# Block 1 linear attention: unpadded queries, 64-row score products in two banks, both token tiles per level

## The chip, the cores and the metric

The kernel runs on one core of a Trainium2 chip. The metric is device microseconds for one call, as a median over runs. Weights and activations come from HBM, and every large product is done in three passes over a high and a low part of its float32 operands.

## The reference, cut to what matters

The model is one block of 256 tokens with a linear-attention mixer, followed by two blocks of softmax attention and SwiGLU. The change is in the first block, in its two linear attentions: `hgrn2` with 4 heads of 64 channels and `gla` with 4 heads of 32 channels, whose values have 64 channels each. Both call this function, with `CHUNK` = 64:

```python
def chunked_gated_linear_attention(q, k, v, log_f):
    # S_t = diag(f_t) S_{t-1} + k_t v_t^T ; o_t = S_t^T q_t, chunkwise
    def step(state, inp):
        qi, ki, vi, gi = inp
        cum = jnp.cumsum(gi, axis=2)
        diff = cum[:, :, :, None, :] - cum[:, :, None, :, :]
        decay = jnp.where(causal, jnp.exp(jnp.where(causal, diff, 0.0)), 0.0)
        scores = jnp.einsum('bhid,bhijd,bhjd->bhij', qi, decay, ki)
        ...
f = lb + (1.0 - lb) * jax.nn.sigmoid(z)                          # hgrn2: log_f = log f
log_f = jax.nn.log_sigmoid((g_lr @ w_g_up + b_g)) / 16.0         # gla: g_lr has 16 columns
```

So the score of query i and key j is the sum over channels of q·k·exp(cum_i − cum_j), for j ≤ i. Beside it the block has an RG-LRU mixer (a convolution of 4 taps, two block-diagonal products, a scan), output gates, and one output projection `w_out` over all three.

## The kernel before, in words

The 256 tokens are two tiles of 128. Channels lie on partitions: `fqz`, `fk` and `cum` hold queries, keys and the running sums of log f (scans, L940) in three blocks of 128 channels, f = 0 and 1 with two `hgrn2` heads each, f = 2 with the four `gla` heads. `fqz` has one slot for each of the 8 heads, with zeros in the channels of the other heads, so that a product over all 128 rows sums over one head alone.

The kernel has no chunk state. It builds the whole triangle of scores `S` for each tile from products that each have a reference time in the middle: for the half-block sizes s = 1, 2, 4, ..., 64 (levels `li` 0 to 6) every block of 2s tokens gives queries of its second half times exp(cum − cum at the middle), and keys of its first half times the inverse. A level of a tile (`level`, called tile-level below) is one subtraction `E` (L1047, GpSimd), two exponentials (ScalarE), the keys `kq` (L1059 or L1062, GpSimd), three queries `qs` (L1067 twice, L1069, VectorE), and products on TensorE (L1073) into one PSUM bank. The four smallest levels multiply all 128 keys by 64 queries and pick what counts by `copy_predicated` into `S` (L1078, VectorE); the others multiply block by block and ScalarE copies (L1081). `diagonal` (L1028, L1030) gives i = j, `across` the queries of tile 1 times the keys of tile 0. `outputs` multiplies `S` by the values (L1104, L1105), norms, gates and transposes.

The order is written by hand as a string, `plan`: `v`, `af`, `cq`, `c`, `lru`, `g`, `o` are projections and the LRU mixer; two digits are a level and a tile; X, D, O are `across`, `diagonal`, `outputs`. `weave` starts a unit at each mark and moves all that are alive one `yield` on. A scheduler then merges the engines' streams by this priority. PSUM has four single banks `mm_t` in a ring, two `acc_t` (projections, convolution, LRU), two `tp_t`. Weights come by `piece`: a load on SP's queue into one of four `raw` buffers, a high part on ScalarE (L108), a low part `wl_t` on VectorE or GpSimd (L111), nine buffers each. A convolution's three taps (L958) read the `acc_t` of its projection, so the bank is free only after the last tap. `evac` copies PSUM out by ScalarE and VectorE in turn. At the end `contract` multiplies by `w_out` in the order [2, 3, 0, 1] of its four pieces, adds, norms (`rms_norm`), and the gated MLP (`gv1` weights) follows.

Of the kernel before, what the change touches and what calls it, by code (L numbers as in the profile page):

```python
# [69 lines left out]
class Net:  # L70
    POOL_SHARE = 3

    def __init__(self, ctx, tc, io):
# [756 lines left out]

    def mixers1(self, mix, post):
# [64 lines left out]
        def af():  # L896
            ks, n = group("af")
            ps = [self.mm.tile([P, 2, T], F32, name="mm_t") for _ in range(2)]
# [16 lines left out]
        def cq():
            ks, n = group("cq")
            ps = self.mm.tile([P, 2, T], F32, name="mm_t")
# [6 lines left out]
            ps = self.mm.tile([P, T], F32, name="mm_t")  # L924
# [3 lines left out]
            ps = self.mm.tile([P, T], F32, name="mm_t")  # L928
# [87 lines left out]
        def scaled(E, q):  # L1016
            w = E.shape[2]
            qa, qc = self.t2(4, w, name="qa"), self.t2(4, w, name="qc")
            v.tensor_tensor(qa.rearrange("p (b j) t -> p b j t", b=2), q[:, 0:4, :].rearrange("p (b j) t -> p b j t", b=2),
                            E[:, 0:2, :].unsqueeze(2).broadcast_to([P, 2, 2, w]), ALU.mult)  # L1020
            v.tensor_tensor(qc, q[:, 4:8, :], E[:, 2:3, :].broadcast_to([P, 4, w]), ALU.mult)
            return qa, qc

        def products(ksrc, qa, qc):
# [6 lines left out]
            return pa, pc  # L1031

        def diagonal(t):
            tsl = slice(t * P, (t + 1) * P)
            ps = products(fk[:, :, tsl], fqz[:, 0:4, tsl], fqz[:, 4:8, tsl])
            yield
            for i, p_ in enumerate(ps):
                v.tensor_tensor(S[:, t, 4 * i : 4 * i + 4, :], p_, self.ident.unsqueeze(1).broadcast_to([P, 4, P]), ALU.mult)

        def level(t, li):  # L1040
            s = LEVELS[li]
            tsl = slice(t * P, (t + 1) * P)
# [23 lines left out]
            for b in range(2):
                v.tensor_tensor(qv[:, 2 * b : 2 * b + 2], q2[:, 2 * b : 2 * b + 2],  # L1067
                                E2[:, b : b + 1].broadcast_to([P, 2, nb, s]), ALU.mult)
            v.tensor_tensor(qv[:, 4:8], q2[:, 4:8], E2[:, 2:3].broadcast_to([P, 4, nb, s]), ALU.mult)  # L1069
            ps = self.mm.tile([P, 8, 64], F32, name="mm_t")  # L1070
            for rows, cols in blocks:
                for f, h0, h1 in ((0, 0, 2), (1, 2, 4), (2, 4, 8)):
                    nc.tensor.matmul(ps[rows, h0:h1, cols], lhsT=kq[:, f, rows], rhs=qs[:, h0:h1, cols],  # L1073
                                     start=True, stop=True)
            yield
            if li < MASKED:
                mk = masks[:, li, :].rearrange("p (b u) -> p b u", u=s).unsqueeze(1).broadcast_to([P, 8, nb, s])
                v.copy_predicated(second(S[:, t]), mk, blk(ps))  # L1078
            else:
                for b, (rows, cols) in enumerate(blocks):  # L1080
                    act.activation(second(S[rows, t])[:, :, b], ps[rows, :, cols], AF.Copy)  # L1081

        def across():
            Eq, Ek = (mix.tile([P, 3, P], F32, name="E", bufs=3) for _ in range(2))
# [4 lines left out]
            kq = mix.tile([P, 3, P], F32, name="kq", bufs=3)  # L1089
            g.tensor_tensor(kq, fk[:, :, 0:P], Ek, ALU.mult)  # L1090
            qa, qc = scaled(Eq, fqz[:, :, P:T])
            ps = products(kq, qa, qc)
            yield
            for i, p_ in enumerate(ps):
                self.evac(SX[:, 4 * i : 4 * i + 4, :], p_)

# [37 lines left out]
        for tok in plan.split():
            if tok in F:
                seq.append(F[tok])
            elif tok in "|-":
                seq.append(None)
            elif tok[0] in U:
                seq += [[U[tok[0]](int(tok[1]))], None]  # L1140
            else:
# [314 lines left out]
```

## Time and profile before

| | us |
|---|---|
| median of 3 runs (1338.17 to 1339.03) | 1338.34 |
| the profiled execution, its own time | 1337.82 |
| its span | 1336.0 |
| TensorE busy in the span | 1296.4 (97%) |
| VectorE busy | 887.6 (66%) |
| ScalarE busy | 729.7 (55%) |
| GpSimd busy | 560.1 (42%) |

The profiled execution takes 1.82 us more than its span (launch and end). Its own time is 0.52 us under the median. Times below count from the span's start. PE is TensorE's matmul, PEld its weight load, DVE VectorE, ACT ScalarE, POOL GpSimd. Block 1's mixers take roughly the first 150 us of the span.

### The profile page before, as it was taken

The page shows a single profiled execution, that of the slowest core. Times are in us where ns is not written, and L with a number is a line of the kernel's source. Part 1 is how long each engine was busy: PE and PEld are TensorE (multiplying, and loading weights), DVE is VectorE, ACT ScalarE, POOL GpSimd, SP SyncE. Part 2 cuts the span into 40 slices and gives each one's busy share as a digit, 9 for nine tenths or more (in the row PEclk, how much of TensorE's full clock was granted, in tenths as well). Part 3 has the DMA queues.
Part 4 walks back from the last instruction along what each step waited for, and adds up shares of the span by engine and source line. Part 5 has one row for each costly group of instructions (what it writes and reads, how often), then busy time and mean ns, then how long its engine had stood idle before and what let it go on. Part 6 is the DMA issues. An engine that isn't in the chain of part 4 may idle for free.

```text
span 1336.0 us, 19335 instructions
## 1 busy us (share of the span) xinstructions
PE 1296.4 (97%) x7028; PEld 1092.1 (82%) x7028; DVE 887.6 (66%) x1402; ACT 729.7 (55%) x1282; POOL 560.1 (42%) x542
## 2 busy tenths in 40 slices
PE   8888999999999999999999999999999999999997
PEld 6767788888888887877888888888887877888886
DVE  5798588863577636587767745677726678777734
ACT  5775466654555543475565543555533666565540
POOL 5563433333444435830534444334436831444430
PEclk9999999999999999999999999999999999999999
DMA  6523555575655564550665565655664540655560
GB/s 221 190 64 124 183 164 187 188 221 156 222 188 186 189 205 134 182 173 1 191 218 188 187 208 152 211 190 189 221 190 129 168 157 1 221 191 188 189 205 32
DMA packets 63922, 227.19 MB, mean 170 GB/s; under 512 B 7105, under 2 KB 8145, under 8 KB 63058
## 3 DMA queue, kind: packets, MB, share of 16 engines
q1 hardware_dynamic: 63826, 225.95, 52.7%
q8 instruction: 55, 0.90, 0.3%
q14 instruction: 41, 0.34, 0.1%
HBM read 224.88 MB, written 1.05 MB: 169 GB/s over the span
## 4 chain that ended last, share of the span: by engine, by line
PE 80%; POOL 6%; DVE 5%; issue 3%; DMA 3%; ACT 2%; SPq 0%; DVEq 0%; ACTq 0%; POOLq 0%
PE mm_t L347 38%; PE acc_t L214 5%; PE acc_t L208 5%; PE acc_t L211 5%; PE mm_t L214 3%; PE mm_t L211 3%; PE mm_t L208 3%; PE mm_t L133 3%; PE mm_t L131 3%; PE mm_t L132 3%; POOL wl_t L111 3%; PE tp_t L149 2%; PE mm_t L431 1%; PE mm_t L684 1%; PE acc_t L131 1%
## 5 line engine op out<-in xcount | busy, mean ns | idle before, releaser
L111 POOL TENSOR_TENSOR wl_t<-raw,wh_t 128x512 fp32r<-128x512 f32 (+3 forms) x270 | 408.6, 1536 | 576.8 <-ACT wh_t L108 570.6
L111 DVE TENSOR_TENSOR wl_t<-raw,wh_t 128x1024 fp32r<-128x1024 f32 (+2 forms) x272 | 391.2, 1445 | 239.8 <-ACT wh_t L108 238.9
L108 ACT ACTIVATE wh_t<-raw 128x1024 fp32r<-128x1024 f32 (+2 forms) x407 | 416.5, 1039 | 222.8 <-PE mm_t L214 135.1
L347 PE MATMUL mm_t<-xx,wh_t 128*128 128x512 f32 x1456 | 429.0, 395 | 0.0
L347 PEld LDWEIGHTS mm_t<-xx,wl_t 128*128 128x128 f32 x1456 | 247.9, 188 | 47.4
L347 PE MATMUL mm_t<-xx,wl_t 128*128 128x256 f32 x1456 | 261.4, 281 | 0.0
L347 PEld LDWEIGHTS mm_t<-xx,wh_t 128*128 128x128 f32 x1456 | 236.2, 189 | 15.7
L350 DVE TENSOR_TENSOR sum<-sum,mm_t 128x256 f32<-128x256 f32 x182 | 75.4, 414 | 38.0 <-ACT sum L349 37.9
L349 ACT ACTIVATE sum<-mm_t 128x256 f32<-128x256 f32 x182 | 67.9, 373 | 43.0 <-PE mm_t L347 43.0
L208 PE MATMUL mm_t<-wh_t,hh 128*128 128x512 f32 x218 | 85.2, 391 | 0.0
L211 PE MATMUL mm_t<-wl_t,hh 128*128 128x512 f32 x218 | 84.8, 389 | 0.0
L211 PE MATMUL acc_t<-wl_t,hh 128*128 128x512 f32 x218 | 84.8, 389 | 0.0
L208 PE MATMUL acc_t<-wh_t,hh 128*128 128x512 f32 x218 | 84.8, 389 | 0.0
L131 PE MATMUL mm_t<-wh_t,xx 128*128 128x512 f32 (+2 forms) x224 | 83.8, 374 | 0.8 <-ACT xx L125 0.7
L132 PE MATMUL mm_t<-wl_t,xx 128*128 128x512 f32 (+2 forms) x224 | 83.0, 371 | 0.0
L133 PE MATMUL mm_t<-wh_t,xx 128*128 128x512 f32 (+2 forms) x224 | 82.0, 371 | 0.0
L125 ACT ACTIVATE hh<-ht 128x256 fp32r<-128x256 f32 x72 | 30.1, 418 | 85.4 <-DVE ht L294 85.4
L214 PE MATMUL acc_t<-wh_t,hl 128*128 128x512 f32 x218 | 71.8, 389 | 0.0
L214 PE MATMUL mm_t<-wh_t,hl 128*128 128x512 f32 x218 | 68.1, 389 | 0.0
L131 PE MATMUL acc_t<-xx,wh_t 128*128 128x256 f32 x176 | 52.2, 297 | 5.0 <-ACT wh_t L108 2.8
L126 DVE TENSOR_TENSOR hl<-ht,hh 128x256 fp32r<-128x256 f32 x72 | 37.9, 526 | 22.1 <-ACT hh L125 22.1
L132 PE MATMUL acc_t<-xx,wh_t 128*128 128x256 f32 x176 | 50.8, 289 | 0.0
(336 smaller groups left out, 2046.0 us busy)
## 6 DMA issues: line engine op xcount, KB each, us to landing
raw<-in_wgu_dram SPq DMA_DIRECT2D x176, 512.0 KB, 4.4
raw<-in_wd_dram SPq DMA_DIRECT2D x109, 512.0 KB, 4.4
raw<-in_gv_dram SPq DMA_DIRECT2D x42, 512.0 KB, 4.5
raw<-in_w_in_dram SPq DMA_DIRECT2D x36, 512.0 KB, 4.4
raw<-in_wo_dram SPq DMA_DIRECT2D x24, 512.0 KB, 3.8
gb<-in_ln_dram SPq DMA_DIRECT2D x6, 1024.0 KB, 4.7
raw<-in_w_in_dram SPq DMA_DIRECT2D x16, 384.0 KB, 3.6
raw<-in_w_in_dram SPq DMA_DIRECT2D x8, 416.0 KB, 3.6
```

What stands on the lines that cost most here:

```text
L108: nc.scalar.activation(hv, raw, AF.Copy)
L111: eng.tensor_tensor(lv[:, x : x + m], raw[:, x : x + m], hv.bitcast(F32)[:, x : x + m], ALU.subtract)
L126: self.nc.vector.tensor_tensor(dst_l, src, dst_h.bitcast(F32), ALU.subtract)
L131: mm(out, lhsT=lhs[0], rhs=rhs[0], start=start, stop=False, **kw)
L132: mm(out, lhsT=lhs[0], rhs=rhs[1], start=False, stop=False, **kw)
L133: mm(out, lhsT=lhs[1], rhs=rhs[0], start=False, stop=stop, **kw)
L208: m = self.nc.tensor.matmul(ps[t][h], lhsT=lh, rhs=wh[:, sl], start=first, stop=False)
L211: self.nc.tensor.matmul(ps[t][h], lhsT=lh, rhs=wl[:, sl], start=False, stop=False)
L214: self.nc.tensor.matmul(ps[t][h], lhsT=ll, rhs=wh[:, sl], start=False, stop=last)
L347: nc.tensor.matmul(out, lhsT=lhsT, rhs=rhs, start=k == 0 and i == 0, stop=k == NK - 2 and i == 3)
L349: nc.scalar.activation(r, ps[:, 1, :], AF.Copy)
L350: nc.vector.tensor_tensor(r, r, ps[:, 0, :], ALU.add)
```

## The change

Queries become `fq` with 4 slots: a slot holds two heads, one on channels 0 to 63 and one on channels 64 to 127 (a `gla` head still has zeros beside it in its 64). `products` runs each score product on 64 rows, the upper and the lower half in turn, and writes the halves' results into the two banks of a double tile (`double`; two of them in the ring, in place of four single banks, for block 1). `level` handles both tiles: one `E`, one `kq` and two `qs` for 256 tokens, all on VectorE, then products per tile. `kq` lives in two fixed buffers that are zeroed once. The heads leave `outputs` in another order. `af` evacuates with one copy in place of two, and the load of `consts` moves ahead on SP's queue. The plan is a new string.

```diff
+    def double(self):
+        return self.mm.tile([P, 2, 512], F32, name="mm_t")
...
-        fqz = mix.tile([P, 8, T], F32, name="fqz")
+        fq = mix.tile([P, 4, T], F32, name="fq")
-        v.memset(fqz, 0.0)
+        v.memset(fq[:, 2:4, :], 0.0)
+        kqs = [mix.tile([P, 3, T], F32, name=f"kq{i}") for i in range(2)]
+        for kq in kqs:
+            g.memset(kq, 0.0)
...
-            fqv = fqz[:, 0:4, :].rearrange("p (b j) t -> p b j t", b=2)
-            for r in range(2):
-                a = slice(r * 64, r * 64 + 64)
-                self.evac(fqv[a, :, r, :], ps[0][a])
+            self.evac(fq[:, 0:2, :], ps[0])
...
-                self.evac(fqz[a, 4 + h, :], ps[a, 0, :], 32.0 ** -0.5)
+                self.evac(fq[a, 2 + h % 2, :], ps[a, 0, :], 32.0 ** -0.5)
...
-            for j in range(2):
-                nc.tensor.matmul(pa[:, 2 * j : 2 * j + 2, :], lhsT=ksrc[:, j, :], rhs=qa[:, 2 * j : 2 * j + 2, :],
-                                 start=True, stop=True)
-            nc.tensor.matmul(pc, lhsT=ksrc[:, 2, :], rhs=qc, start=True, stop=True)
+        FS = ((0, 0, 1), (1, 1, 2), (2, 2, 4))
+        def products(ps, ksrc, qsrc, rows=slice(0, P), cols=slice(0, P)):
+            for f, s0, s1 in FS:
+                for r in range(2):
+                    a = slice(r * 64, r * 64 + 64)
+                    nc.tensor.matmul(ps[rows, 4 * r + s0 : 4 * r + s1, cols], lhsT=ksrc[a, f, rows], rhs=qsrc[a, s0:s1, cols],
+                                     start=True, stop=True)
+        def heads():
+            return self.double().rearrange("p b (s c) -> p (b s) c", s=4)
+        def scale(out, q, E):
+            v.tensor_tensor(out[:, 0:2], q[:, 0:2], E[:, 0:2], ALU.mult)
+            v.tensor_tensor(out[:, 2:4], q[:, 2:4], E[:, 2:3].broadcast_to([P, 2, *E.shape[2:]]), ALU.mult)
...
-        def level(t, li):
+        def level(li):
-            g.tensor_tensor(E.rearrange("p f (b u) -> p f b u", u=2 * s), c4d,
-                            c4d[:, :, :, s - 1 : s].broadcast_to([P, 3, nb, 2 * s]), ALU.subtract)
+            E = mix.tile([P, 3, T], F32, name="E", bufs=3)
+            v.tensor_tensor(view(E), c4d, c4d[:, :, :, s - 1 : s].broadcast_to([P, 3, NT * nb, 2 * s]), ALU.subtract)
...
+            self.nkq += 1
+            kq = kqs[self.nkq % 2]
+            qs = mix.tile([P, 4, P], F32, name="qs", bufs=3)
+            v.tensor_tensor(first(kq), first(fk), first(E), ALU.mult)
+            scale(blk(qs), second(fq), second(E))
...
+            for t in range(NT):
+                ps = heads()
+                for rows, cols in blocks:
+                    products(ps, kq[:, :, t * P : (t + 1) * P], qs[:, :, t * 64 : (t + 1) * 64], rows, cols)
...
-            g.tensor_tensor(Ek, cum[:, :, 0:P], cum[:, :, P - 1 : P].broadcast_to([P, 3, P]), ALU.subtract)
+            v.tensor_tensor(Ek, cum[:, :, 0:P], cum[:, :, P - 1 : P].broadcast_to([P, 3, P]), ALU.subtract)
...
-        plan = ("v0 af cq X0 c0 D0 v1 40 c3 60 c1 c2 lru 50 30"
-                " | 20 00 g0 10 O0 D1 o0 61 31 41 o1 51 11 o2 g1 o3 21 01 O1")
+        plan = "v0 af cq X0 c0 D0 D1 v1 L4 c3 L6 c1 c2 lru L5 L3 | L2 g0 L0 o0 L1 o1 g1 O0 o2 O1 o3"
...
+        mm1 = ExitStack()
+        self.mm = mm1.enter_context(tc.tile_pool(name="mm1", bufs=2, space=PSUM))
...
+        mm1.close()
+        self.mm = self.ctx.enter_context(tc.tile_pool(name="mm", bufs=4, space=PSUM))
         tc.keep_in_program_order(nc.sync.dma_start(ctile, io["consts"]))
```

TensorE of the kernel before, where the gate's small matmul stands (`mm_t_531<-glr`, from which the `gla` decays come) among the projections of convolution 0 (`acc_t_577`) and of the values of tile 1 (`acc_t_622`):

```order
L132 MATMUL acc_t_622<-wl_t_142,xx_94 128x512
L133 MATMUL acc_t_622<-wh_t_141,xx_94 128x512
L131 MATMUL acc_t_622<-wh_t_149,xx_94 128x512
L133 MATMUL acc_t_577<-xx_94,wl_t_567 128x256
L131 MATMUL acc_t_577<-xx_94,wh_t_573 128x256
L929 MATMUL mm_t_531<-glr_529,gup_196 128x256
L132 MATMUL acc_t_577<-xx_94,wh_t_573 128x256
L133 MATMUL acc_t_577<-xx_94,wl_t_574 128x256
```

TensorE after, at the same matmul, now among the projections of convolution 3 (`acc_t_667`), with products of the diagonal (`mm_t_606`) behind it:

```order
L131 MATMUL acc_t_667<-xx_91,wh_t_566 128x256
L132 MATMUL acc_t_667<-xx_91,wl_t_567 128x256
L130 MATMUL acc_t_667<-xx_91,wh_t_566 128x256
L131 MATMUL acc_t_667<-xx_91,wh_t_566 128x256
L936 MATMUL mm_t_531<-glr_529,gup_195 128x256
L1030 MATMUL mm_t_606<-fq_252,fk_253 128x128 x4
L1030 MATMUL mm_t_606<-fq_252,fk_253 128x256 x2
L132 MATMUL acc_t_667<-xx_91,wl_t_567 128x256
L130 MATMUL acc_t_667<-xx_91,wh_t_573 128x256
L131 MATMUL acc_t_667<-xx_91,wh_t_573 128x256
```

The gate's matmul now has 33 more projection matmuls ahead of it on TensorE than before (22 of 128x256, 11 of 128x512): convolution 0 and the values of tile 1 are complete, and 17 matmuls of convolution 3 are issued. Convolution 3 writes into the `acc_t` bank from which the taps of convolution 0 read.

VectorE before, from the scans (`cum`) on; `xc` are taps of a convolution, `qa` and `qc` the queries of `across`:

```order
L940 SCALAR_TENSOR_TENSOR cum_255<-keepm_200,cum_255 128x128 x2
L1019 TENSOR_TENSOR qa_613<-fqz_253,E_547 128x512
L1021 TENSOR_TENSOR qc_614<-fqz_253,E_547 128x512
L958 SCALAR_TENSOR_TENSOR xc1_260<-acc_t_656,pp_92,xc1_260 128x253
L958 SCALAR_TENSOR_TENSOR xc1_260<-acc_t_656,pp_92,xc1_260 128x254
L958 SCALAR_TENSOR_TENSOR xc1_260<-acc_t_656,pp_92,xc1_260 128x255
L1067 TENSOR_TENSOR qs_691<-fqz_253,E_648 128x128 x2
L1069 TENSOR_TENSOR qs_691<-fqz_253,E_648 128x256
L958 SCALAR_TENSOR_TENSOR xc0_259<-acc_t_708,pp_92,xc0_259 128x253
L1067 TENSOR_TENSOR qs_828<-fqz_253,E_685 128x128 x2
```

VectorE after, from the scans on:

```order
L947 SCALAR_TENSOR_TENSOR cum_254<-keepm_199,cum_254 128x128 x2
L1091 TENSOR_TENSOR E_548<-cum_254 128x3x128
L1058 TENSOR_TENSOR E_661<-cum_254 128x768
L965 SCALAR_TENSOR_TENSOR xc0_262<-acc_t_754,pp_89,xc0_262 128x253
L1037 TENSOR_TENSOR qs_613<-fq_252,E_547 128x256
L1038 TENSOR_TENSOR qs_613<-fq_252,E_547 128x256
L110 TENSOR_TENSOR wl_t_1047<-raw_1044,wh_t_1046 128x1024
L965 SCALAR_TENSOR_TENSOR xc0_262<-acc_t_754,pp_89,xc0_262 128x254
L1097 TENSOR_TENSOR kq0_256<-fk_253,E_548 128x3x128
L1058 TENSOR_TENSOR E_696<-cum_254 128x768
L110 TENSOR_TENSOR wl_t_1053<-raw_1050,wh_t_1052 128x1024
L1067 TENSOR_TENSOR kq1_257<-fk_253,E_661 128x24x16
```

`E` and `kq` are now in VectorE's stream, `qs` comes once for two tiles, and taps stand between them.

TensorE before, levels 3 and 2 of tile 0 (`mm_t_864`, `mm_t_885`) beside the LRU's second half (L970):

```order
L1073 MATMUL mm_t_864<-qs_860,kq_858 128x128 x2
L970 MATMUL acc_t_779<-xc0_259,bd_198 64x256 x4
L1073 MATMUL mm_t_864<-qs_860,kq_858 128x256
L1073 MATMUL mm_t_885<-qs_881,kq_879 128x128 x2
L1073 MATMUL mm_t_885<-qs_881,kq_879 128x256
L970 MATMUL acc_t_787<-xc1_260,bd_198 64x256 x4
L970 MATMUL acc_t_800<-xc1_260,bd_198 64x256 x4
L1073 MATMUL mm_t_952<-qs_948,kq_946 128x128 x2
L1073 MATMUL mm_t_952<-qs_948,kq_946 128x256
```

TensorE after, level 3 of tile 1 (`mm_t_945`) and level 2 of tile 0 (`mm_t_1023`) among projections of `o0` (`acc_t_1063`):

```order
L132 MATMUL acc_t_1063<-xx_91,wl_t_1040 128x256
L130 MATMUL acc_t_1063<-xx_91,wh_t_1046 128x256
L1030 MATMUL mm_t_945<-qs_934,kq0_256 128x64 x4
L1030 MATMUL mm_t_945<-qs_934,kq0_256 128x2x64 x2
L1030 MATMUL mm_t_1023<-qs_1019,kq1_257 128x64 x4
L1030 MATMUL mm_t_1023<-qs_1019,kq1_257 128x2x64 x2
L131 MATMUL acc_t_1063<-xx_91,wh_t_1046 128x256
L132 MATMUL acc_t_1063<-xx_91,wl_t_1047 128x256
L130 MATMUL acc_t_1063<-xx_91,wh_t_1046 128x256
```

The six products of a tile-level are four of 64 columns and two of 2x64 columns, and here two tile-levels stand back to back; before, a tile-level was three (two of 128 columns, one of 256), and each tile had its own keys `kq`; now `kq0` and `kq1` serve both tiles of every other level.

## Rows read from the trace of the kernel before

**Rows 1.** Busy time by stretch: us from:to, length, engines, clock, DMA share, GB/s

```profile
60.00:70.00 10.00, 7.81 (x51) 6.78 (x51) 9.91 (x16) 7.33 (x14) 8.05 (x10) 0.83 0.19 54
70.00:80.00 10.00, 6.42 (x62) 3.57 (x59) 9.95 (x15) 6.42 (x19) 8.53 (x8) 0.88 0.67 210
84.00:124.80 40.80, 38.91 (x283) 34.46 (x282) 38.86 (x68) 25.70 (x51) 19.37 (x18) 1.00 0.07 21
124.80:147.40 22.60, 19.70 (x86) 15.21 (x85) 12.28 (x19) 10.37 (x15) 6.22 (x5) 1.00 0.48 174
```

**Rows 2.** What PE waited for, 0 to 165 us: total us, times, longest

```profile
PE mm_t L1073 <- DVE qs L1067: 3.4, 3, 2.1
...
PE acc_t L131 <- ACT wh_t L108: 2.8, 1, 2.8
PE acc_t L131 <- DVE xc L958: 2.2, 1, 2.2
PE acc_t L208 <- DVE gg L1008: 1.9, 1, 1.9
```

**Rows 3.** VectorE groups, 45 to 118 us: count, busy us, mean ns, idle before

```profile
L1067 DVE TENSOR_TENSOR qs<-fqz,E 128x128 f32<-128x128 f32 x28 | 12.0, 463 | 0.0
L111 DVE TENSOR_TENSOR wl_t<-raw,wh_t 128x1024 fp32r<-128x1024 f32 x7 | 10.8, 1537 | 3.5 <-ACT wh_t L108 3.5
L1069 DVE TENSOR_TENSOR qs<-fqz,E 128x256 f32<-128x256 f32 x14 | 9.3, 666 | 0.0
```

**Rows 4.** GpSimd groups, 45 to 118 us

```profile
L1047 POOL TENSOR_TENSOR E<-cum 128x384 f32<-128x384 f32 x14 | 12.9, 925 | 12.5 <-DVE qs L1069 11.2 <-DVE qc L1021 1.3
...
L1059 POOL TENSOR_TENSOR kq<-fk,E 128x384 f32<-128x384 f32 x8 | 8.9, 1118 | 2.1 <-ACT E L1051 1.4 <-POOL E L1047 0.5 <-PE mm_t L1073 0.3
```

**Rows 5.** Lines 1067 and 1069: count, ns min/median/max

```profile
L1067 DVE TENSOR_TENSOR qs<-fqz,E x28: 259/281/1085, 63.4 to 108.7; 128x128 f32<-128x128 f32 x28
...
L1069 DVE TENSOR_TENSOR qs<-fqz,E x14: 407/414/1483, 64.6 to 109.7; 128x256 f32<-128x256 f32 x14
```

**Rows 6.** TensorE in time: start, us, line, shape, count (an f32 matmul gives two)

```profile
69.84 1.20 PE L1073 MATMUL mm_t<-qs,kq 128*16 128x32 f32 x28
...
82.09 1.95 PE L970 MATMUL acc_t<-xc,bd 64*64 64x256 f32 x16
...
97.72 2.00 PE L1105 MATMUL mm_t<-vt,gb 128*128 128x64 f32 x16 [0.59 <-DVE gb L1078]
...
108.57 2.37 PE L1073 MATMUL mm_t<-qs,kq 128*128 128x128 f32 x16
```

**Rows 7.** What the weight loads (PEld) waited for, 60 to 125 us

```profile
PEld mm_t L1073 <- issue: 1.7, 4, 0.8
...
PEld acc_t L970 <- issue: 0.9, 4, 0.3
```

**Rows 8.** TensorE in time, single instructions

```profile
46.92 0.69 PE L929 MATMUL mm_t<-glr,gup 16*128 16x256 f32 x2
...
85.84 0.58 PE L131 MATMUL acc_t<-wh_t,xx 128*128 128x512 f32 x1
...
91.28 0.39 PE L133 MATMUL acc_t<-wh_t,xx 128*128 128x512 f32 x1
```

**Rows 9.** ScalarE in time

```profile
50.03 0.47 ACT L931 ACTIVATE gy<-mm_t,pp 128x256 f32<-128x256 f32 x1
```

**Rows 10.** VectorE in time

```profile
57.14 2.29 DVE L940 TENSOR_TENSOR_SCAN cum<-keepm,cum 128x128 f32<-128x128 f32 x2
...
79.14 0.41 DVE L1069 TENSOR_TENSOR qs<-fqz,E 128x256 f32<-128x256 f32 x1
79.47 0.47 DVE L958 SCALAR_TENSOR_TENSOR xc<-acc_t,pp,xc 128x255 f32<-128x255 f32 x1
```

**Rows 11.** Chain of waits, 140 to 165 us: start, us, what

```profile
151.72 5.93 DMA raw<-in_gv_dram
```

**Rows 12.** Loads issued: out<-in, queue, op, count, KB, median us to landing

```profile
raw<-in_gv_dram SPq DMA_DIRECT2D x42, 512.0 KB, 4.5
```

More of the change, by code (lines that the diff above doesn't have):

```diff
@@ L897, in af @@
             ks, n = group("af")
-            ps = [self.mm.tile([P, 2, T], F32, name="mm_t") for _ in range(2)]
+            pd = self.double()
+            ps = [pd[:, i].rearrange("p (j t) -> p j t", j=2) for i in range(2)]
             for j in range(4):
                 self.proj_feat(ks, ps[j // 2][:, j % 2, :], lambda w, j=j: w[:, j * P : (j + 1) * P])
-            fqv = fqz[:, 0:4, :].rearrange("p (b j) t -> p b j t", b=2)
-            for r in range(2):
-                a = slice(r * 64, r * 64 + 64)
-                self.evac(fqv[a, :, r, :], ps[0][a])
+            self.evac(fq[:, 0:2, :], ps[0])
             sg, sn = self.t2(2, T, name="sg"), self.t2(2, T, name="sn")
@@ L916, in cq @@
             ks, n = group("cq")
-            ps = self.mm.tile([P, 2, T], F32, name="mm_t")
+            pd = self.double()
+            ps = pd[:, 0].rearrange("p (j t) -> p j t", j=2)
             for j in range(2):
@@ L927, in cq @@
             self.evac(glr, ps[0:16])
-            ps = self.mm.tile([P, T], F32, name="mm_t")
+            ps = self.double()[:, 0, :T]
             nc.tensor.matmul(ps, lhsT=gup, rhs=glr, start=True, stop=True)
@@ L1033, in diagonal @@
         def diagonal(t):
             tsl = slice(t * P, (t + 1) * P)
-            ps = products(fk[:, :, tsl], fqz[:, 0:4, tsl], fqz[:, 4:8, tsl])
+            ps = heads()
+            products(ps, fk[:, :, tsl], fq[:, :, tsl])
             yield
-            for i, p_ in enumerate(ps):
-                v.tensor_tensor(S[:, t, 4 * i : 4 * i + 4, :], p_, self.ident.unsqueeze(1).broadcast_to([P, 4, P]), ALU.mult)
-        def level(t, li):
+            for i in range(2):
+                v.tensor_tensor(S[:, t, 4 * i : 4 * i + 4, :], ps[:, 4 * i : 4 * i + 4, :],
+                                self.ident.unsqueeze(1).broadcast_to([P, 4, P]), ALU.mult)
@@ L1041, in level @@
+        def level(li):
             s = LEVELS[li]
-            tsl = slice(t * P, (t + 1) * P)
-            q = fqz[:, :, tsl]
             nb = P // (2 * s)
-            c4d = cum[:, :, tsl].rearrange("p f (b u) -> p f b u", u=2 * s)
-            E = mix.tile([P, 3, P], F32, name="E", bufs=3)
-            g.tensor_tensor(E.rearrange("p f (b u) -> p f b u", u=2 * s), c4d,
-                            c4d[:, :, :, s - 1 : s].broadcast_to([P, 3, nb, 2 * s]), ALU.subtract)
+            view = lambda a: a.rearrange("p f (b u) -> p f b u", u=2 * s)
+            first = lambda a: view(a)[:, :, :, :s]
+            second = lambda a: view(a)[:, :, :, s:]
+            blk = lambda a: a.rearrange("p f (b u) -> p f b u", u=s)
+            c4d = view(cum)
+            E = mix.tile([P, 3, T], F32, name="E", bufs=3)
+            v.tensor_tensor(view(E), c4d, c4d[:, :, :, s - 1 : s].broadcast_to([P, 3, NT * nb, 2 * s]), ALU.subtract)
@@ L1066, in level @@
[L1066 to L1074, printed above, removed]
@@ L1075, in level @@
-            yield
[L1076 to L1081, printed above, removed]
+            pss = []
+            for t in range(NT):
+                ps = heads()
+                for rows, cols in blocks:
+                    products(ps, kq[:, :, t * P : (t + 1) * P], qs[:, :, t * 64 : (t + 1) * 64], rows, cols)
+                pss.append(ps)
@@ L1083, in across @@
+            yield
+            for t, ps in enumerate(pss):
+                if li < MASKED:
+                    mk = masks[:, li, :].rearrange("p (b u) -> p b u", u=s).unsqueeze(1).broadcast_to([P, 8, nb, s])
+                    v.copy_predicated(second(S[:, t]), mk, blk(ps[:, :, :64]))
+                else:
+                    for b, (rows, cols) in enumerate(blocks):
+                        act.activation(second(S[rows, t])[:, :, b], ps[rows, :, cols], AF.Copy)
         def across():
-            Eq, Ek = (mix.tile([P, 3, P], F32, name="E", bufs=3) for _ in range(2))
+            Eq, Ek = (mix.tile([P, 3, T], F32, name="E", bufs=3)[:, :, :P] for _ in range(2))
@@ L1092, in across @@
-            ps = products(kq, qa, qc)
+            kq = kqs[0]
+            self.nkq = 0
+            qs = mix.tile([P, 4, P], F32, name="qs", bufs=3)
+            v.tensor_tensor(kq[:, :, 0:P], fk[:, :, 0:P], Ek, ALU.mult)
+            scale(qs, fq[:, :, P:T], Eq)
+            ps = heads()
+            products(ps, kq, qs)
             yield
-            for i, p_ in enumerate(ps):
-                self.evac(SX[:, 4 * i : 4 * i + 4, :], p_)
+            for i in range(2):
+                self.evac(SX[:, 4 * i : 4 * i + 4, :], ps[:, 4 * i : 4 * i + 4, :])
@@ L1099, in outputs @@
             yield
-            po = self.mm.tile([P, 512], F32, name="mm_t")
+            po = self.double()[:, 0]
             for h in range(8):
-                hsl = slice(h * 64, (h + 1) * 64)
+                r, i = divmod(h, 4)
+                c = 2 * i + r if i < 2 else 2 + 2 * r + i
+                hsl = slice(c * 64, (c + 1) * 64)
                 if t == 1:
@@ L1129, in mixers1 @@
             F[f"o{j}"] = lambda j=j: lru_out(j)
-        U = {"X": lambda t: across(), "D": diagonal, "O": outputs}
-        plan = ("v0 af cq X0 c0 D0 v1 40 c3 60 c1 c2 lru 50 30"
-                " | 20 00 g0 10 O0 D1 o0 61 31 41 o1 51 11 o2 g1 o3 21 01 O1")
+        U = {"X": lambda t: across(), "D": diagonal, "O": outputs, "L": level}
+        plan = "v0 af cq X0 c0 D0 D1 v1 L4 c3 L6 c1 c2 lru L5 L3 | L2 g0 L0 o0 L1 o1 g1 O0 o2 O1 o3"
         seq = []
@@ L1226, in run @@
         nc.gpsimd.memset(ones, 1.0)
-        w = []
+        mm1 = ExitStack()
+        self.mm = mm1.enter_context(tc.tile_pool(name="mm1", bufs=2, space=PSUM))
+        wps = self.double()
+        w = [wps[:, h] for h in range(2)]
         for h in range(2):
-            ps = self.mm.tile([P, 512], F32, name="mm_t")
-            nc.tensor.matmul(ps, lhsT=ones, rhs=row[:, h * 512 : (h + 1) * 512], start=True, stop=True)
-            w.append(ps)
+            nc.tensor.matmul(w[h], lhsT=ones, rhs=row[:, h * 512 : (h + 1) * 512], start=True, stop=True)
         self.spread(self.rms_norm(0, w, 1e-6), 0)
```

29 lines of the change are left out of this document (2 added, 27 removed).

## The prediction

> **What bounds the kernel now.** Read the engines' shares first: TensorE is busy for nearly the whole span, so a change counts by the matmul time it takes away and by the stops of TensorE that it ends or makes. Then the table by stretches [rows 1]. From 60 to 80 us, while the decays are built, TensorE is busy 7.81 and 6.42 us of each 10, its clock falls to 0.83 and 0.88 of the upper level, and VectorE is at 9.91 and 9.95: there VectorE sets the pace. From 84.0 to 124.8 (scores, gates, LRU outputs, up to the last `outputs` matmul) TensorE does 38.91 of 40.80 and VectorE 38.86: both are full, and the loads stand almost still (DMA share 0.07) since the buffers are full. From 124.8 to 147.4 (`contract`) TensorE idles 2.9. Third, the waits of TensorE [rows 2]: for `qs` 3.4 us in three stops, for a weight's high part 2.8, for the taps that hold an `acc_t` bank 2.2, and in `contract` for `gg` 1.9. All other stages are untouched but for a swap of ScalarE and VectorE in later PSUM copies (one `evac` fewer); I put that, and the first 22 us, at nothing, ±2, as TensorE is busy throughout there and both engines have idle time.
>
> **A. VectorE and GpSimd.** The 28 + 14 `qs` instructions, 12.0 + 9.3 us [rows 3], go, and so do GpSimd's `E` (14 of 925 ns) and `kq` (8 of 1,118 ns in this window, with more behind it) [rows 4]. The means of `qs` are inflated: the medians are 281 and 414 ns, the minima 259 and 407 [rows 5]. They give 148 ns for 128 more elements: 1.16 ns an element on 111 ns. By that an `E` of 768 takes 1.0 us, `kq` of 384 0.56, a `qs` of 256 0.41: 2.4 per level, 16.7 for seven, 1.9 for `across`, 18.6 in all. Against 21.3 plus 1.4 for the `qa`, `qc` of `across` (two of 512 at 0.70) VectorE wins 4.1. Its seven `wl_t` of 1,024 elements take 1,537 ns each [rows 3] against 1.30 by the same line; I take that they lose the difference, 1.7, when GpSimd no longer runs its 28 instructions beside them. If the stretch stays, an element costs up to 463/259 = 1.8 times as much, and the 18.6 become 29 (+10.6). I take the lower end: the median row, not the mean, is what most instructions show even now.
>
> **B. Score products.** A full-row product of 8 matmul rows and 1,280 columns takes 2.37 [rows 6] (at 108.57): 1.85 ns a column. A tile-level (512 columns) is 0.95, a `diagonal` or `across` (1,024) 1.9. Now each is three pairs on 64 rows. Whether the two of a pair run together, the nearest row says: the LRU's 64-row products, 8 of 256 columns, took 1.95 [rows 6] (at 82.09), 0.24 each, half of 256 × 1.85 = 0.47. They use a quarter of the array each, the new ones a half, so it isn't the same thing. A floor lies under short matmuls: with 128 weight columns 8 matmuls of 64 columns took 2.00 [rows 6] (at 97.72), 0.25 each; with 16 weight columns 14 took 1.20 [rows 6] (at 69.84), 0.086 each. Paired, a masked tile-level is 3 × 0.25 = 0.75, a full product 0.25 + 0.25 + 0.47 = 0.97, s = 64 about 0.5, s = 32 about 0.58, s = 16 (4 blocks × 3 pairs × 0.086) 1.03. Unpaired, a masked tile-level is 6 × 0.25 = 1.5, s = 32 1.2, s = 16 2.1. Over all 17 products: 18.9 before; 12.9 paired (−6.0), 25.8 unpaired (+6.9). I take paired.
>
> Changes of shape cost something: at products and LRU matmuls the weight load stood 8 times for 1.7 + 0.9 with no cause shown [rows 7], 0.33 each. There will be some 14 more, since tile-levels stand among projections singly: up to 4.6. Most of the pause lies beside a running matmul; I take a third, 1.5, of it 0.5 in the last stage. The Trainium skill (TensorEngine Tiling (Array Packing), Key Properties) has both sides: tiles operate independently, weight load and matmul in parallel, which would bring pairs to half; and a change of mode drains the engine. The 0.24 of the LRU's matmuls agrees with the first, the 0.33 with the second; charged in full, the second would add 3.1 to the sum.
>
> **C. The decays: start to LRU.** The gate's matmul is at 46.92 [rows 8] and gets 33 projection matmuls ahead. From 85.84 to 91.28 [rows 8] 23 steps of 512 columns take 5.44: 0.237 each, half for 256. So 22 × 0.118 + 11 × 0.237 = 5.2, its own 0.69, and a wait: convolution 3 needs the bank that the taps of convolution 0 hold. Such stops were 2.2 and 2.8 [rows 2]; I take 2.4. `gy` starts at 46.92 + 5.2 + 0.7 + 2.4 = 55.2, in place of 50.03 [rows 9]. From there to the scans' end (57.14 + 2.29 = 59.43 [rows 10]) it was 9.4; a `wl_t` (1.3) and a copy of values (0.7) no longer stand in between: 7.4, so 62.6. This term is a loss of 3.2 by itself.
>
> Behind the scans VectorE does, up to the last tap, by the order: `E` of 384 (0.56), five `E` (5.0), three `kq` (1.7), eight `qs` (3.3), three 512-element copies (2.1), three `wl_t` (3.9), six taps (2.6): 19.2 in 29 instructions. Neighbours overlap: the `qs` at 79.14 lasts 0.41, and the tap starts at 79.47 [rows 10], 0.08 early. At most 28 × 0.08 = 2.2; I take 1.7. The last tap ends at 62.6 + 17.5 = 80.1, before at 79.94. But before, products of three tile-levels of sizes 8 and 4 and a copy stood ahead of the LRU's second half, which came at 82.09; now nothing but s = 64 does, so 80.3: −1.8.
>
> **D. From there to the last `outputs`**: 40.8 before. Products left then: nine tile-levels (8.6) and `diagonal` (1.9), 10.5; now eight masked (6.0), two of s = 32 (1.2), one of s = 64 (0.5), 7.7: −2.8. Shape changes +0.5. The waits of 1.9 (40.80 − 38.91) grow: there are two PSUM pairs and two `kq` buffers, and a level's tile must wait for the copy of the one before the last. Six such hand-overs at 0.5, 3.0 in all, +1.1. The price lies between 0 and the longest `qs` wait, 2.1 [rows 2]; most waits in this stage are near 0.5. Sum −1.2.
>
> **E. `contract`**: of its 2.9 idle the 1.9 for `gg` [rows 2] came because `o3` ran just ahead of it. Now `o3`'s elementwise work has `outputs` of tile 1 beside it, but the transposes of O0 and O1 come close: idle 1.0, −1.9. Ends: −2.9 and +1.0 (one more such wait).
>
> **F.** The chain waits for a `gv1` load of 5.93 [rows 11], where the median is 4.5 [rows 12]; the load of `consts` beside it moves ahead. −0.5 (0 to −1.4).
>
> Sum: −1.8 − 1.2 − 1.9 − 0.5 = −5.4. From the profiled execution's 1337.82: 1332.4; that is 0.52 under the median of the runs, so **1332.9**.
>
> **The rivals.**
> 1. More of it shows: the gate's wait for a bank (2.4) doesn't come, since c0's taps are now done early, the hand-overs don't grow (1.1) and shape changes are hidden (0.5): 1332.9 − 4.0 = 1328.9; with the 1.5 of shorter `wl_t` before the scans, 1327.4. For it: VectorE is freed by 4.1 where it is full. Against: two-tile steps make the chain from scans to scores longer.
> 2. The pairs don't run together. For it: the floor of 0.25 belongs to the weight load, whose 128 columns don't shrink with rows. Then D has 8 × 0.75 + 2 × 0.6 = 7.2 more, of which the hand-over waits swallow 1.0: 1339.1. The Trainium skill (TensorE: Matmul & The Clock Gate, LDWEIGHTS (loading the stationary operand)) says that a load's time goes by its columns, 32×128 like 128×128. No row here shows a 64-row load of 128 columns beside another.
> 3. What is won is given back at the next load: a `contract` that starts earlier finds its loads, idle in D for want of buffers, not earlier, and E, F and D's gain fall away: 1332.9 + 3.6 = 1336.5. For it: the chain at 151.72 is a load [rows 11]. Against: DMA share 0.48 in that stretch [rows 1].
> 4. Slower: the hand-overs. TensorE is in order; if it stands at each of the six for the whole chain of copy, `kq`, `qs`, each is like the longest `qs` wait, 2.1, not 0.5: 6 × 1.5 = 9 more, 1341.9, with projections queued behind. It decides from 1.4 each (0.5 + 5.4/6). Against: four to eleven projection matmuls (0.5 to 2.6 us) stand between most tile-levels.
>
> **How the numbers follow.** Forecast 0.42 (its own range 1329.5 to 1336), more of it 0.17, no pairs 0.14, given back 0.14, hand-overs 0.13. A measurement of this kernel can tell 0.2% (2.7 us) from no change: 1335.7 to 1341.0 is the same. Faster: 0.41 + 0.17 + 0.04 = 0.62. Same: 0.01 + 0.13 + 0.10 + 0.02 = 0.26. Slower: 0.01 + 0.11 = 0.12. Range 1326.5 to 1340.5: it leaves out most of the slower case and the lower tail of the first rival.
>
> **What would show it.** In the profile after: six matmuls of a masked tile-level within 0.75 (1.5 if unpaired); the gate's matmul near 54.5 and the scans' end near 62.6; `qs` of 256 near 0.41 and `wl_t` near 1.3; the LRU's second half at 80.3; stops of TensorE of about 3 us from there to the last `outputs` matmul, which ends near 121.8; about 1 us idle in `contract`. Wrong would be: scans after 65, stops above 7 us in D, or a masked tile-level over 1 us.

## The result, and the profile after

The changed kernel takes 1352.13 us (median of 4 runs, 1348.88 to 1356.4) against 1338.57: a ratio of 1.0097, 95% interval 1.0082 to 1.0112. It is slower by 13 us, where 5.4 less was forecast.

Where the time went is read from one landmark, the transposes of `y` that begin a stage. Behind the output projection of block 1 (row at 161.25 below, before 160.86) and before the first softmax block the two kernels are 0.4 us apart. These are the landmarks around that block, before and then after: its start, the end of its attention, the next stage.

```profile
533.52 1.29 PE L149 MATMUL tp_t<-ident,y 128*128 128x128 f32 x8
...
641.22 0.60 PE L149 MATMUL tp_t<-ident,y 128*128 128x128 f32 x4
...
656.20 1.03 PE L149 MATMUL tp_t<-ident,y 128*128 128x128 f32 x8
```

```profile
533.94 1.29 PE L148 MATMUL tp_t<-ident,y 128*128 128x128 f32 x8
...
652.93 1.04 PE L148 MATMUL tp_t<-ident,y 128*128 128x128 f32 x8
...
668.57 1.03 PE L148 MATMUL tp_t<-ident,y 128*128 128x128 f32 x8
```

So 12 of the 12.9 us of the spans' difference arise between 534 and 669 us, in code that the change doesn't touch. TensorE of the changed kernel, then its stretches of block 1 (as [rows 1]):

```profile
54.44 0.69 PE L936 MATMUL mm_t<-glr,gup 16*128 16x256 f32 x2
55.06 1.15 PE L1030 MATMUL mm_t<-fq,fk 64*128 64x128 f32 x12
...
77.42 0.76 PE L1030 MATMUL mm_t<-qs,kq 64*16 64x16 f32 x48 [4.75 <-DVE SX L477]
...
81.81 1.73 PE L977 MATMUL acc_t<-xc,bd 64*64 64x256 f32 x14 [0.25 <-DVE xc L965]
...
103.63 0.94 PE L1030 MATMUL mm_t<-qs,kq 64*128 64x64 f32 x12
...
161.25 1.29 PE L148 MATMUL tp_t<-ident,y 128*128 128x128 f32 x8 [2.59 <-DVE y L778]
```

```profile
60.00:70.00 10.00, 6.47 (x60) 5.67 (x58) 8.90 (x19) 9.62 (x15) 1.70 (x1) 1.00 0.40 124
70.00:80.00 10.00, 3.69 (x66) 1.92 (x64) 10.00 (x16) 5.28 (x14) 4.16 (x2) 0.71 0.50 159
83.75:128.20 44.45, 39.43 (x348) 34.56 (x345) 34.94 (x53) 28.80 (x47) 2.52 (x2) 0.92 0.23 71
128.20:148.40 20.20, 19.51 (x90) 15.88 (x89) 10.43 (x19) 7.29 (x12) 9.34 (x7) 1.00 0.32 117
```

The LRU's second half is near its old place (81.81, before 82.09), the stage behind it is 3.65 us longer than before (44.45 against 40.80) at a mean clock of 0.92, and `contract` 2.4 shorter. TensorE's waits, 0 to 180 us (as [rows 2]):

```profile
PE tp_t L148 <- DVE y L778: 6.9, 2, 4.3
PE mm_t L1030 <- DVE SX L477: 4.8, 1, 4.8
...
PE mm_t L1030 <- ACT gb L1086: 2.5, 1, 2.5
...
PE acc_t L130 <- ACT gm L982: 2.5, 1, 2.5
```

The first softmax block, two stretches of before and then of after:

```profile
575.00:590.00 15.00, 15.00 (x117) 14.07 (x116) 11.24 (x30) 10.36 (x29) 5.61 (x8) 1.00 0.64 211
...
620.00:640.00 20.00, 19.75 (x115) 15.48 (x114) 15.37 (x41) 11.68 (x28) 4.51 (x5) 1.00 0.06 12
```

```profile
575.00:590.00 15.00, 15.00 (x98) 13.52 (x98) 10.34 (x24) 7.89 (x20) 5.23 (x8) 0.89 0.66 205
...
620.00:640.00 20.00, 17.13 (x85) 13.43 (x84) 12.17 (x50) 9.04 (x32) 1.19 (x2) 0.83 0.00 0
```

TensorE's waits after, 533 to 669 us:

```profile
PE acc_t L130 <- DVE qf L479: 2.5, 1, 2.5
PE mm_t L672 <- DVE mx L379: 1.6, 1, 1.6
PE acc_t L130 <- DVE wq L479: 1.6, 1, 1.6
PE tp_t L148 <- DVE do L712: 1.2, 1, 1.2
PE tp_t L148 <- ACT pts L424: 0.7, 1, 0.7
```

These are 7.6 us against 1.7 before. The lower clock comes on top: 15 us at a mean of 0.89 and 20 us at 0.83 of the upper level lose at most 1.65 + 3.4, by estimate (less where TensorE stood idle at the lower level). Together 5.9 + 5.05 = 11 of the 12 us.

### The profile page after: what moved, and what is told of

The parts are those of the page before. It is cut to its first block, busy times and chain, and to the rows that moved or that the text cites. A ratio compares the mean times of both kernels' runs of the same rounds, so it can differ in the third digit from the quotient of the medians.

```text
span 1348.9 us, 19525 instructions
## 1 busy us (share of the span) xinstructions
PE 1297.1 (96%) x7178; PEld 1094.1 (81%) x7178; DVE 883.7 (66%) x1389; ACT 729.4 (54%) x1268; POOL 533.9 (40%) x514
## 4 chain that ended last, share of the span: by engine, by line
PE 84%; POOL 5%; DVE 3%; issue 2%; DMA 2%; ACT 2%; SPq 0%; DVEq 0%; ACTq 0%; POOLq 0%
PE mm_t L346 38%; PE acc_t L207 5%; PE acc_t L213 5%; PE acc_t L210 5%; PE mm_t L207 3%; PE mm_t L213 3%; PE mm_t L210 3%; PE mm_t L132 3%; PE mm_t L130 3%; PE mm_t L131 3%; PE tp_t L148 2%; PE acc_t L130 2%; PE acc_t L131 2%; PE acc_t L132 2%; POOL wl_t L110 1%
```

## Experiments: the loss in the softmax block

`af` calls `evac` once less, so ScalarE and VectorE change places in all later PSUM copies. Runs a_flip and b_flip put that turn right in the changed kernel, and wrong in the kernel before:

```diff
         self.weave(seq)
+        self.flip ^= 1
```

> The changed kernel with one line more: evac's turn is flipped once after block 1, so that ScalarE and VectorE copy in the two softmax blocks the same PSUM tiles as in the kernel before. Theory P (the loss of some 12 us sits in the first softmax block, 533 to 656 us before and 534 to 669 after, and comes from the flipped turn of the copies alone): 1339 to 1341, the stretch between those transposes back near 123 us. Rival M (the loss there comes from PSUM pools opened anew, the moved load of consts, or another placement in memory): 1350 to 1353, no change. Rival S (both softmax blocks share it evenly): about 1345.

> The kernel before with the same one line after block 1, nothing else. Theory P: +11 to +13, 1350, all of it in the first softmax block. Rival M: 1338.5, no change. If it is in between, the loss needs the changed block 1 as well.

Measured against the kernel before: a_flip 0.9979 (0.9966 to 0.9993), b_flip 1.0102 (1.0087 to 1.0118). Theory P holds both ways: the turn costs 13 to 16 us with either block 1, and without it the change is faster by 2.8 us. From landmark to landmark the block takes 122.10 us in a_flip (before 122.68) and 136.30 in b_flip (after 134.63), so Rival S falls too. How the loss begins, in b_flip, is read from VectorE and then TensorE:

```profile
557.72 2.27 DVE L111 TENSOR_TENSOR wl_t<-raw,wh_t 128x1024 fp32r<-128x1024 f32 x1 [3.04 <-ACT wh_t L108]
559.91 1.22 DVE L154 TENSOR_SCALAR ms<-ms 128x2 f32<-128x2 f32 x1
561.05 0.18 DVE L545 COPY kr<-mm_t 128x32 f32<-128x32 f32 x1
561.15 0.47 DVE L480 TENSOR_SCALAR wq<-acc_t,ctile 128x256 f32<-128x256 f32 x1
```

```profile
561.67 0.39 PE L131 MATMUL acc_t<-xx,wh_t 128*128 128x256 f32 x1 [2.86 <-DVE wq L480]
```

The copy of `wq` stands behind a weight's low part and a small `ms`; the bank is free only when it ends, and the projections behind it wait. In the kernel before ScalarE did it at 558.34. The clock did not fall behind this stop (1.00 from 563.5 to 573.5); it fell later, to means of 0.83 and 0.73 over the 10 us from 573.5 and from 623.5.

Which copies matter was tried by swapping parts of the 31 of that block. a_qf and b_qf name the engine of some copies in the call; a_qf does so in the changed kernel, its turn left as it is, and by that also moves one `wq` of the second softmax block. The others swap by the number of the copy:

```diff
-        if self.flip:
+        self.cnt = getattr(self, "cnt", 0) + 1
+        if self.flip ^ (self.cnt in SWAP):
```

> The changed kernel (turn of the copies as it is, flipped), but in the first softmax block the copies of the first wq tile and of the two qf tiles are done on ScalarE, as in the kernel before; all other copies stay flipped. Theory Q (these copies, behind weights and behind a wait for GpSimd in VectorE's queue, hold projection banks; that makes the 2.9 and 2.5 us stops of TensorE and with the low clock behind them most of the 13 us): 1338 to 1343. Rival T (the loss sits in the tail of the attention units, 605 to 641 us, where pts, dk and mqk copies changed engines too): 1347 to 1352.

> The kernel before, with only these four copies swapped in the first softmax block (first wq tile and both qf on VectorE, second wq tile on ScalarE); the order of the other work stays as it is in all but a few places. Theory Q: +8 to +13, 1347 to 1352. Rival T: within 3 us of 1339.

> The kernel before with 13 of the 31 copies of the first softmax block on the other engine: the projections' wq, wk, qf, kf, mlv and mqk. The scheduler's order of TensorE then differs from before in that block, but isn't the one of the fully flipped kernel. Theory first half (the projection banks held by late copies start the loss): +7 to +12, 1346 to 1351. Theory order (the loss needs the one order in which no output projections stand between the attention units from 614 to 630 us): +2 to +4, 1341 to 1343.

> The kernel before with the other 10 copies of that block swapped: dk, dq and pts of the differential attention. Theory tail (the copies inside the attention chain, on a full VectorE, make the stops at mx, do and pts): +5 to +8, 1344 to 1347. Theory first half: within 2 us of 1339. Theory order: within 3 us of 1339, and the two halves' losses don't add up to the 13 us of the whole.

> The kernel before with nine copies of the first softmax block on the other engine: wk, kf, mlv and mqk; wq and qf stay as they were. Theory together (the loss needs the late wq and qf copies on VectorE, each stopping TensorE with the low clock behind it, and VectorE filled by the other copies makes qf late): within 3 us of the kernel before. Theory by themselves: +8 to +10.

| run | copies on the other engine | ratio to before (95%) |
|---|---|---|
| a_qf | all but first wq and both qf of the block (in the changed kernel) | 1.0020 (1.0010 to 1.0031) |
| b_qf | both wq, both qf | 1.0014 (1.0004 to 1.0023) |
| b_first | wq, qf, wk, kf, mlv, mqk | 1.0081 (1.0057 to 1.0105) |
| b_second | dk, dq, pts | 1.0017 (1.0007 to 1.0027) |
| b_rest | wk, kf, mlv, mqk | 1.0064 (1.0039 to 1.0090) |

b_first and b_second (23 of the 31 copies; the other eight, of `axv`, `axq`, `axk` and `wdv`, were not tried) add up to nearly the whole (+10.9 and +2.3 of 13.7), so the first half carries it. It does so in another way than in the changed kernel, though: b_first's trace has no stops for `mx` and `do`, and its clock is 1.00 from 620 to 640 and 0.77 from 575 to 590. My theory Q fell: b_qf gives 1.9 us, and the stop at `wq` of 2.9 is in its trace too. b_rest, without `wq` and `qf`, still costs 8.6, so "together" fell as well. a_qf, which recovers 10 of the 13 us, speaks for the same copies as Q; that would be no contradiction if each edit also gives the scheduler another order, which was not tested apart. Two more runs took the rest apart:

> The kernel before with one copy swapped in the first softmax block: wk, of 128x256, to ScalarE. One copy is 0.4 us of work, but the scheduler then gives TensorE another order there, nearly that of b_rest. Theory order: +5 to +9, close to b_rest's +7 to +8. Theory load (which engine does how many copies): within 1.5 us of the kernel before.

> The kernel before with the other eight copies of b_rest swapped (kf, mlv, mqk), wk as it was; TensorE's order stays nearly that of before. Theory order: within 2 us of the kernel before. Theory load: +5 to +9.

b_wk: 1.0056 (1.0037 to 1.0075), 7.4 us for one copy of 0.4 us. b_kf8: 1.0032 (1.0018 to 1.0046), 4.3 us, between what its two theories said; its trace shows no new stop above 0.2 us and no lower clock, so where this comes from is open. The two don't add up to b_rest (11.7 against 8.6). ScalarE and TensorE of b_wk, and TensorE's next stretch:

```profile
572.78 2.00 ACT L109 ACTIVATE wh_t<-raw 128x1024 fp32r<-128x1024 f32 x2
574.67 0.37 ACT L478 ACTIVATE wk<-acc_t 128x256 f32<-128x256 f32 x1
```

```profile
575.10 1.31 PE L661 MATMUL mm_t<-wk,wq 64*128 64x256 f32 x4 [1.84 <-ACT wk L478]
```

```profile
575.00:590.00 15.00, 14.90 (x79) 12.07 (x80) 10.98 (x26) 8.21 (x21) 5.99 (x9) 0.77 0.67 212
```

`wk` waits behind two weight copies, TensorE stops 1.84 us, and the next 15 us run at 0.77 of the upper clock, a loss of 3.45: 5.3 of the 6.1 us by which that stretch is longer in the profiled run. The order of TensorE in the block differs as well, and what that adds was not separated. Nor does the low clock always follow the stop. b_rest's profiled run stops for `wk` as long, and its clock stays at the upper level:

```profile
575.37 1.13 PE L661 MATMUL mm_t<-wk,wq 64*128 64x256 f32 x4 [1.95 <-ACT wk L478]
```

```profile
575.00:590.00 15.00, 14.63 (x101) 12.74 (x102) 12.80 (x28) 9.79 (x24) 6.45 (x9) 1.00 0.71 212
```

Its block is only 3.3 us longer than before, with eight more copies swapped. a_qf's profiled run has the stop too (1.93) and no low clock. The runs of b_wk spread in the same way: one took 1340.25 at a mean clock of 0.995 over the whole span, the four others 1344.01 to 1347.84 at 0.990 or 0.991. This fits a price of some 3 us without the low clock and 4 to 8 more with it. The clock falls in some executions and not in others; what decides is not shown.

## Experiments: block 1

> The changed kernel with the norm weights of the first norm in two PSUM tiles in place of two halves of one double tile. In the changed kernel's trace the first transposes stand at 11.59 us, before at 7.21; VectorE has the low part of a weight ahead of y, and that waits for a load. Theory D (y waits for both halves of the double tile, so the scheduler puts it behind the weight): transposes back near 7.2, the gate's matmul some 3 us earlier, and 2 to 4 us of it kept to the end: 1348 to 1350. Rival L (loads, not y, set the pace to the gate's matmul): the transposes come early, but the end stays within 1 us of 1352.

> Both edits of a_flip and a_start. Theory P with D: 1335 to 1338, that is 1 to 4 us under the kernel before, since block 1 itself then shows what the forecast summed up in part (its last stages were some 4 us shorter from 11.6 us on). If the start's 4 us are not kept: 1339 to 1341.

```diff
-        wps = self.double()
-        w = [wps[:, h] for h in range(2)]
+        w = [self.double()[:, 0] for _ in range(2)]
```

The first `y` goes ahead of the weight again and the first transposes are at 7.06 (a_both) in place of 11.59. a_start 1.0081 (1.0068 to 1.0093) is 2 us under the changed kernel, as theory D had it; a_both 0.9980 (0.9972 to 0.9989) is level with a_flip, as Rival L had it. Both intervals overlap those of the kernels without the edit, so between 0 and 2 of those 4 us reach the end. In a_both's trace the gate's matmul, the LRU's second half and the gates behind it are:

```profile
52.23 0.69 PE L936 MATMUL mm_t<-glr,gup 16*128 16x256 f32 x2
...
80.10 2.00 PE L977 MATMUL acc_t<-xc,bd 64*64 64x256 f32 x16
...
88.53 0.80 PE L130 MATMUL acc_t<-wh_t,xx 128*128 128x512 f32 x1 [4.42 <-ACT gm L982]
```

So 1.7 us come through to the LRU (80.10 against 81.81), and the stop for `gm` behind it takes them back: 4.42 in place of 2.48.

> The changed kernel with the turn put right (as a_flip, 1337.1), and the products of a tile issued half by half: three on channels 0 to 63, then three on 64 to 127, in place of in turn. Theory pairs (neighbours on different rows run together): a full product goes from 1.04 us back towards 1.9, a masked tile-level from 0.94 to 1.2 to 1.5; the end +1 to +5. Rival (each matmul goes by its own floor, neighbours don't matter): products as they were, end within 1 us of a_flip.

```diff
-            for f, s0, s1 in FS:
-                for r in range(2):
+            for r in range(2):
+                for f, s0, s1 in FS:
```

1.0006 (0.9995 to 1.0018), some 3.6 us over a_flip. Two products of TensorE in a_unpair; the changed kernel's are 1.15 and 0.94 above:

```profile
53.84 1.47 PE L1030 MATMUL mm_t<-fq,fk 64*128 64x128 f32 x12
...
103.42 1.21 PE L1030 MATMUL mm_t<-qs,kq 64*128 64x64 f32 x12
```

Pairs do overlap, by less than half.

> As a_flip, with both copies of SX on ScalarE (before one of them on VectorE, where it stands behind a weight's low part and an E). Theory hand-over (the 4.6 us stop of TensorE for SX at 71 to 76 us comes from two PSUM pairs and that copy, and sets when the LRU starts): stop gone or below 2 us, end -2 to -4 against a_flip. Rival VectorE (the last tap on VectorE, near 80.4, sets the LRU's second half; the stop is slack): the stop moves to the next copies on VectorE (the diagonal's), the end within 1 us of a_flip.

```diff
-                self.evac(SX[:, 4 * i : 4 * i + 4, :], ps[:, 4 * i : 4 * i + 4, :])
+                act.activation(SX[:, 4 * i : 4 * i + 4, :], ps[:, 4 * i : 4 * i + 4, :], AF.Copy)
```

0.9988 (0.9978 to 0.9998). The stop of 4.6 became three, 6.8 us in all, the last at the diagonal's copies, as the rival had it:

```profile
71.49 0.64 PE L1030 MATMUL mm_t<-qs,kq 64*16 64x16 f32 x48 [1.43 <-ACT SX L1103]
75.15 0.77 PE L1030 MATMUL mm_t<-qs,kq 64*16 64x16 f32 x48 [2.00 <-ACT gb L1086]
79.26 0.90 PE L1030 MATMUL mm_t<-qs,kq 64*64 64x64 f32 x9 [3.35 <-DVE gb L1046]
```

> As a_flip, with the two-tile E subtraction and kq of the seven levels on GpSimd, where they were before, in place of VectorE; VectorE loses 7 x (0.95 + 0.55) = 10.5 us of work. Theory A (the move to VectorE pays, since a level's chain on GpSimd, some 1.8 + 1.1 us, is longer than on VectorE and slows its neighbours): +2 to +6, 1339 to 1343. Rival (VectorE is what is full from 60 to 80 us): the last tap comes 3 to 5 us earlier, end -2 to -5, 1332 to 1335.

1.0032 (1.0020 to 1.0044), 7 us over a_flip: the move to VectorE pays. TensorE's waits there grow:

```profile
PE mm_t L1030 <- DVE SX L477: 5.6, 1, 5.6
PE mm_t L1030 <- ACT gb L1086: 4.9, 2, 4.0
PE mm_t L1030 <- DVE kq L1097: 3.9, 1, 3.9
```

> As a_flip, with both square roots of the LRU held back on ScalarE until the tanh of its second half are issued; two table loads of 1.28 us go as well. In a_flip TensorE stops 2.5 us at 87 to 89 us for a bank that such a tanh holds, behind the first half's root, and runs at the low clock behind it. Theory D (that stop and its clock are what ate the forecast's gain from the LRU to the last outputs): the first gates matmul 2 to 4 us earlier, the end 3 to 6 us under a_flip, 1331 to 1334. Rival (the stage is held by VectorE's chain of levels, the stop is slack): the stop moves to a later wait, the end within 1.5 us of 1337.

```diff
+                        last = act.activation(gm[:, q, :], ps[:, q, :], AF.Tanh, bias=bh[:, 4 * m + j : 4 * m + j + 1], scale=0.5)
...
+                            last0 = act.activation(gm[:, q, :], gm[:, q, :], AF.Tanh, bias=cj, scale=cj)
...
-                act.activation(ts[2 * i], ts[2 * i], AF.Sqrt, scale=0.0625)
+                rt = act.activation(ts[2 * i], ts[2 * i], AF.Sqrt, scale=0.0625)
+                self.follow(rt, last)
+                self.follow(rt, last0)
```

0.9984 (0.9972 to 0.9996): no gain at the end. Its stop for `gm` fell to 1.2 us, and from the LRU's second half to the last `outputs` its profiled run takes 40.8 us where a_flip's takes 44.9. But that run's LRU came 3.9 us later than a_flip's (83.52 against 79.62), its gate's matmul already 3.2 later (55.86 against 52.70). So the missing gain doesn't show that the stop was slack.

> The changed kernel with the turn put right, the first norm's weights in two tiles and both square roots behind the tanh of the LRU's second half. If the stage from the LRU to the output projection is what was missing in the gain: 1332 to 1335 where the kernel before has 1339, ratio 0.995 to 0.9975. If it is given back at the next loads: 0.998 as in a_flip, a_both and a_gm.

0.9974 (0.9965 to 0.9983), 3.5 us under the kernel before, the best version measured; its interval overlaps a_flip's, so what the added edits bring isn't shown.

## Why the prediction was wrong, point by point

- **The step that failed** is in the first part: "All other stages are untouched but for a swap of ScalarE and VectorE in later PSUM copies (one `evac` fewer); I put that, and the first 22 us, at nothing, ±2, as TensorE is busy throughout there and both engines have idle time." The swap cost 13.7 us (b_flip). Idle time of an engine over a stage says nothing about where one copy stands in its queue: a copy that TensorE waits for, be it for the bank (`wq`) or for what it holds (`wk`), stops it when 2 us of other work stand ahead, and the clock can fall behind the stop. Which copies make the whole 13.7 us, and by which path, stays open. None of the rivals held it, and none of the signs of being wrong came (scans 63.6, stops in D 5.0, a masked tile-level 0.94): they all lie in block 1. In the first 22 us, put at nothing in the same sentence, the first transposes came 4.4 us late (11.59, before 7.21).
- **A** was right in its sizes, `E` 1.04, `kq` 0.55 and `qs` 0.415 us each (below), and a_Ekq_pool shows that, for two-tile steps, the move earns 7 us. `wl_t` kept its mean (1.53), but five of the nine took 1.22 to 1.23, under the 1.30 assumed. Those of 2.29 and 2.34, at 72.96 and 115.20, lie beside a `wl_t` of GpSimd; so does one of 1.22 at 68.74, so the cause isn't shown. The upper bound of 29 doesn't follow from its factor (1.8 on the element part of 18.6 gives 30.5); it enters no sum. VectorE groups after, 45 to 118 us (as [rows 3]):

```profile
L110 DVE TENSOR_TENSOR wl_t<-raw,wh_t 128x1024 fp32r<-128x1024 f32 x9 | 13.8, 1530 | 4.8 <-ACT wh_t L107 4.8
L1058 DVE TENSOR_TENSOR E<-cum 128x768 f32<-128x768 f32 x7 | 7.3, 1044 | 0.0
L1067 DVE TENSOR_TENSOR kq<-fk,E 128x384 f32<-128x384 f32 x7 | 3.8, 546 | 0.0
L1037 DVE TENSOR_TENSOR qs<-fq,E 128x256 f32<-128x256 f32 x8 | 3.3, 415 | 0.0
```

- **B**: paired was right, against rival 2, but with less gain: a full product 1.04 to 1.15 (0.97 forecast, 1.9 before), a masked tile-level 0.94 alone and 0.80 where two follow each other (0.75 forecast; before 0.95 by the forecast's sum, 1.04 alone at 91.52). Rival 2 had a right reason: a load of 128 weight columns took 182 to 188 ns on 64 rows and 192 on 128. But pairs overlap all the same.
- **C**: the gate's matmul came at 54.44 (near 54.5 forecast), and this was luck: the wait of 2.4 for a bank ahead of it didn't come, as rival 1 said, and the late start stood in for it. With the start put right it comes at 52.23 (a_both). The scans ended 1.0 us late, the last tap 1.65, the LRU's second half 1.5 (81.81). The gain of 1.8 shrank to 0.3, with the start 4 us late; in a_both it is 2.0.
- **D** was mis-sized, and in sign: −1.2 forecast, +3.65 measured. The stops were 2.5 for `gb` and 2.5 for `gm` on ScalarE, 5.0 in all, where six of 0.5 had been assumed. Behind them the gates ran at the lower clock, which had no term: their steps of 512 columns took 0.43 us there and 0.23 later, some 2 us over ten steps. The stretch from 88 to 94 us:

```profile
88.00:94.00 6.00, 4.26 (x10) 3.39 (x11) 2.68 (x7) 5.97 (x14) 0.00 (x0) 0.50 0.00 0
```

- **E** −2.4 (−1.9 forecast) and **F** (148.43 to 161.25, 12.8 against 13.45 before, −0.6; −0.5 forecast) were right in size.
- With the turn put right the change gives −2.8 (a_flip), half of the forecast. By the changed kernel's trace D (4.9 worse than forecast) and C (1.5) are what is missing: at the end of block 1 nothing of the 5.4 is left (161.25 against 160.86). Rival 4 named hand-overs, and those for `SX` of 4.75 and for `gb` of 2.5 came, but with `SX` moved (a_sx) the stops moved on and the end stayed. Rival 3 is open: a_gm's stop went and the end stayed, but its LRU came late as well.

## What to carry to other kernels

An edit that changes a count on which later code takes turns (copies, weight parts) is a change of all that code: compare the order and the engine of every copy behind it, and put the turn back if nothing else asks for it. Look at the copies that TensorE waits for, and at what stands ahead of each on its engine. In the profiled runs the block with a stop of 1.9 us for one such copy was 6.1 us longer where the clock fell behind it (b_wk) and 2.3 to 3.3 where it didn't (a_qf, b_rest). Forecast such stops with the low clock behind them as a price of its own, and with a chance.

## What the runs showed of the hardware

- One copy of 0.4 us on the other engine made 7.4 us (b_wk); behind a stop of 1.84 us the granted clock was 0.77 over the next 15 us, and behind one of 1.95 us for the same copy it was 1.00 (b_rest).
- Products on 64 rows in turn overlap in part: 0.94 us against 1.21 half by half, 1.15 against 1.47.
